# A table of ones moves from the constants to the projections' pool, and every tile on the left side of SBUF begins 96 bytes lower

## The chip, the cores and the metric

The kernel runs on one NeuronCore of a Trainium2 chip. The metric is the device time of one execution in microseconds (us). Each engine has its own instruction stream: TensorE multiplies matrices (PE in the profile, and PEld for its weight loads), VectorE (DVE) and ScalarE (ACT) work element by element, GpSimd (POOL) has a few odd jobs here, and SyncE (SP) issues the DMAs between HBM and SBUF. SBUF is the on-chip memory of 128 partitions; a tile takes the same range of bytes in each of them. PSUM takes the results of TensorE.

## The reference

Two decoder layers on one sequence of 1024 tokens with 1024 features, everything in float32. Layer 0 mixes tokens by sparse attention (an indexer scores all keys, each query keeps the best 256, then grouped attention with 16 query heads and 4 key heads of 64), layer 1 by a gated convolution of width 3. After each mixer comes a SwiGLU network with 2816 hidden features.

```python
for i in range(DEPTH):
    mod = c_act @ ada_w[i] + ada_b[i]
    sh1, sc1, g1, sh2, sc2, g2 = [m[:, None, :] for m in jnp.split(mod, 6, axis=-1)]
    h = _rmsnorm(x, norm1_g[i]) * (1.0 + sc1) + sh1
    y = _dsa_mixer(...) if i % 2 == 0 else _short_conv_mixer(...)
    x = x + g1 * y
    h = _rmsnorm(x, norm2_g[i]) * (1.0 + sc2) + sh2
    x = x + g2 * _swiglu(h, ffn_w_gate[i], ffn_w_up[i], ffn_w_down[i])

def _rmsnorm(x, g):      # used for q and k as well, over the 64 features of a head
    xf = x.astype(jnp.float32)
    y = xf * lax.rsqrt(jnp.mean(xf * xf, axis=-1, keepdims=True) + NORM_EPS)
```

## The kernel before, in words

**Layout and products.** Activations lie transposed, features on the partitions and tokens along the row, in two halves of 512 tokens. A float32 product is made of three fp32r products (`mm3`): each operand is split into a high part (a copy that rounds to fp32r, on ScalarE) and a low part (the rest, a subtraction on VectorE). The weights' parts are the tiles `whi` and `wlo`, a ring of four units each in the pool `w`; each unit is 512 columns wide, that is four 128x128 blocks, and feeds 12 matmuls. In a matmul the block of weights is loaded first (the stationary operand), and 512 columns of activations then stream past it (the moving operand). A profile's row such as `ps_g<-t,whi` names the result in PSUM, then the moving tile, then the stationary one.

**Stages.** `Attention.first_norm` and `project` make queries, keys, values and the indexer's operands (to about 294 us of the profiled span), with activations in `hhi` and `hlo`. `attend` runs the attention for eight blocks of 128 queries, and beside it the output projection (`out_tile`, moving `ohi` and `olo`), to about 622 us. `Tail.run` has the rest: the first SwiGLU network, the convolution, and the second network. There the products go by Strassen-like schemes (`Pair.done`, `down_pairs`) whose moving operands are `h11`, `h21`, `h22`, `t1` to `t4` (named `h` and `t` in rows), and `ph11` (named `ph`). In `down_pairs` the steps `m1`, `m6`, `m3`, `m5` and `m7` take the moving operand's parts from `ph`, and the steps `m2` and `m4` take them from the ring of units, so there both operands are named `whi` or `wlo`. `down` (the convolution's output projection) likewise streams units for the first half of the tokens, and for the second half parts that lie in the memory of `h22` and `t1` (rows with `rh` and `rt`).

**Order of the work.** Every instruction is first recorded and then placed by a planner (`Plan`), which keeps a clock for each engine and issues the recorded operation that can start soonest, smaller `pri` first. What it decides is fixed when the program is built.

**Places in SBUF.** A pool on the left side is put behind the pools that are open there, from low addresses upwards; a pool on the right side (`w`, `keep`, `sel`, `h`, `o`) is counted from the other end. The pool `const` is opened first, and so stands in front of all other pools of the left side: `k4` (keys), `pj` (the projections' scratch tiles), `at` (attention's), and in the tail `x2`, `u`, `h2`, `t2` and `s2`. A tile's length is rounded up to 32 bytes a partition.

**The table of ones.** `rope_pair` needs the sum of squares of each head. It multiplies the squares (`qsq`) by `blk4`, a 128x32 table that has a column of ones for each block of 32 partitions. The table is made in `setup` by one memset to zero and four memsets to one, in the pool `const`. Beside it lies `nss`, 4 numbers a partition for the tail's norms.

Of the kernel before, what the change touches and what calls it, by code (L numbers as in the profile page):

```python
# [9 lines left out]
F32 = mybir.dt.float32  # L10
# [553 lines left out]
P = 128  # L564
# [31 lines left out]
def blk(b):  # L596
    return slice(b * P, (b + 1) * P)


class Trunk:  # L600
# [111 lines left out]
    def setup(self, cz, c, positions, ada_b, n1, n2, conv_w, gq, gk, lg, lb, rope_c, arenas, kgb, freq):  # L712
        nc, cp = self.nc, self.cp
        self.ident = ident = cp.tile([P, P], F32, name="ident")
        nc.gpsimd.memset(ident, 1.0)
        nc.gpsimd.affine_select(ident, ident, pattern=[[-1, P]], compare_op=ALU.is_equal,
                                fill=0.0, base=0, channel_multiplier=1)
        self.nss = cp.tile([P, 4], F32, name="nss")
        self.blk4 = cp.tile([P, 32], F32, name="blk4")
        nc.vector.memset(self.blk4, 0.0)  # L720
        for i in range(4):
            nc.vector.memset(self.blk4[32 * i:32 * i + 32, i:i + 1], 1.0)
        rc = arenas[0].part_of(0)[0:9, P:2 * P]
        for r0, n, v in ((0, 8, c.rearrange("o (k p) -> (o k) p", p=P)), (8, 1, rope_c)):
            nc.scalar.dma_start(rc[r0:r0 + n, :], v)
        pv = self.ps("mm")
        nc.tensor.transpose(pv[:, 0:9], rc, ident[:9, :9])
        self.cact = cp.tile([P, 8], F32, name="cact")
        nc.scalar.activation(self.cact, pv[:, 0:8], AF.Silu)
        nc.vector.tensor_copy(cz[:, :, 0], self.cact)  # L730
        nc.vector.tensor_copy(freq, pv[:, 8:9])
        self.plan.pri = 1.0
        rows, rowb = arenas[0].part_of(1)[:, 0:P], arenas[1].part_of(0)[0:96, 0:P]
        nc.vector.memset(rows, 0.0)
        for r0, n, v in ((R_N1, 16, n1.rearrange("l (k p) -> (l k) p", p=P)),
                         (R_N2, 16, n2.rearrange("l (k p) -> (l k) p", p=P)),
                         (R_CW, 24, conv_w.rearrange("o w (k p) -> (o w k) p", p=P))):
            nc.sync.dma_start(rows.part_of((1, r0))[r0:r0 + n, :], v)
        nc.sync.dma_start(rowb, ada_b.rearrange("l (k p) -> (l k) p", p=P))
        g = arenas[1].part_of(96)[96:98, 0:HD]  # L740
        for r, v in enumerate((gq, gk)):
            nc.sync.dma_start(g[r:r + 1], v)
        for i, r in enumerate(R_G):
            nc.vector.tensor_copy(
                rows.part_of((1, r))[r:r + 2].rearrange("p (r q) -> p r q", q=32),
                g[:, 32 * i:32 * i + 32].unsqueeze(1).to_broadcast([2, 4, 32]))
        self.vec = vec = cp.tile([P, P], F32, name="vec")
        pv = self.ps("mm")
        read = [1] + [(1, r) for r in (R_N1, R_N2, R_CW, *R_G)]
        nc.tensor.transpose(pv[:, 0:P], rows.part_of(read), ident)  # L750
        nc.vector.tensor_copy(vec, pv[:, 0:P])
        self.adab = cp.tile([P, 96], F32, name="adab")
        pb = self.ps("mm")
        nc.tensor.transpose(pb[:, 0:96], rowb, ident[:96, :96])
        nc.vector.tensor_copy(self.adab, pb[:, 0:96])
        self.plan.pri = 27.0
        self.kgb = kgb.rearrange("p (a d) -> p a d", d=HD)
        for i, v in enumerate((lg, lb)):
            nc.sync.dma_start(self.kgb.part_of(i)[:, i], v.to_broadcast([P, HD]))
        mod = cp.tile([P, 2, 6, 8], F32, name="mod")  # L760
        self.mod = [[mod.part_of((i, j))[:, i, j] for j in range(6)] for i in range(2)]
        aff = cp.tile([P, 2, 2, 8], F32, name="aff")
        self.aff = [[aff.part_of((i, j))[:, i, j] for j in range(2)] for i in range(2)]
# [160 lines left out]
class Attention:  # L924
# [42 lines left out]


    def first_norm(self, x, positions, setup):
        tk, nc, plan, sp = self.tk, self.nc, self.plan, self.pj  # L970
        self.C, self.S = (self.hp.tile([P, T], F32, name=v) for v in "CS")
        plan.pri = 0.0
        cz = self.score[7][:, 0:HW].part_of("c").rearrange("p (k m) -> p k m", m=HD)
        nc.vector.memset(cz, 0.0)
        setup(cz, (self.C, self.S))
        self.kp.tile([P, 32], F32, name="pad")
        xt = [self.kp.tile([P, KT, HW], F32, name="xt%d" % i, tag="k%d" % i) for i in range(NH)]
# [101 lines left out]
    def project(self):  # L1079
        tk, nc, sp, plan = self.tk, self.nc, self.pj, self.plan  # L1080
# [2 lines left out]
            "p (h t) -> p h t", h=IH // 2)  # L1083
        self.ssk = sp.tile([P, TB, KVH], F32, name="ssk", bufs=1)
        self.wiT = sp.tile([P, TB, IH], F32, name="wiT", bufs=1)
        n, s, ends = HD + IH, 0, []
        kw = self.s4()
        self.plan.pri = self.KI_W
# [58 lines left out]
        for b in range(TB):  # L1147
            ps = tk.ps("mm", "gemm")[:, 0:KVH * HD]
# [19 lines left out]
    def rope_pair(self, w, half, ts, col, ss, s):  # L1168


        tk, nc, sp = self.tk, self.nc, self.pj
        n = ts.stop - ts.start
        ab, sqs = [], []
        for two in range(2):
            self.unit(s)
            ps = tk.gemm_tile(w[two], P, self.h[half], ts=ts)
            t = sp.tile([P, HW], F32, name="rt", tag="rt")[:, 0:n]
            if col is None:
                self.plan.copy(t, ps)
            else:  # L1180
                c = R_G[two] + col
                nc.scalar.activation(t, ps, AF.Copy, scale=tk.vec[:, c:c + 1])
            if ss is not None:
                sq = sp.tile([P, HW], F32, name="qsq", tag="t2")
                nc.scalar.activation(sq, ps, AF.Square)
                sqs.append(sq)
            ab.append(t)
            s += 1
        if ss is not None:
            ps = tk.ps("mm", "sq")  # L1190
            self.plan.matmuls([(ps.part_of(g)[32 * g:32 * g + 32, 0:P], tk.blk4, sq[:, blk(g)])
                               for sq in sqs for g in range(4)], 3.5e-3, side=4)
            row = sqs[0][:, 0:P]
            self.plan.copy(row, ps.part_of([0, 1, 2, 3])[:, 0:P])
            sm = ps.part_of("n")[:, P:P + 16]
            nc.tensor.matmul(sm, row, tk.ident.rearrange("p (g q) -> p g q", q=32)[:, :, 0:4],
                             start=True, stop=True)
            nc.vector.tensor_copy(ss[:, half * 4:half * 4 + 4, :],
                                  sm.rearrange("p (t n) -> p t n", n=4))
        sl = slice(half * HW + ts.start, (half + 1) * HW)  # L1200
        tmp = [sp.tile([P, HW], F32, name="sw", tag="sw")[:, 0:n] for _ in range(2)]
        tk.rotate(ab, tmp, self.C[:, sl], self.S[:, sl])
        return ab, sl, s
# [892 lines left out]
```

## Time and profile before

| what | value |
|---|---|
| median of 3 runs | 2287.76 us (2282.33 to 2289.04) |
| the profiled execution's own time | 2281.89 us |
| its span, first to last instruction | 2280.1 us |
| PE busy | 2228.1 us, 98% of the span |
| DVE busy | 1903.0 us, 83% |
| ACT busy | 1138.9 us, 50% |
| DMA, q1 | 350.48 MB, 48.5% of 16 engines' span |

A row of a grouped view reads: line, engine, operation, output tile, inputs, shapes, count, then the busy time in us and the mean of one in ns, then the engine's idle time ahead of these instructions and what ended it. Matmuls overlap and their ends are modelled, so the mean duration of one is longer than the time from one start to the next. The rate at which TensorE goes is therefore read from starts: from the timeline, or from the number of matmuls in a window.

### The profile page before, as it was taken

What the parts mean: (1) busy time and instruction counts of PE and PEld (TensorE: products, weight loads), DVE (VectorE), ACT (ScalarE), POOL (GpSimd) and SP (SyncE); (2) the same over time, 40 slices, a digit from 0 to 9 for tenths busy, and PEclk for the clock granted to TensorE, in tenths of its full rate; (3) what the DMA queues carried; (4) which work ended last, traced back from release to release, by engine and by line L of the source; (5) the groups of instructions that cost most, each with busy time, mean ns of one, the idle gap of its engine ahead of it and who ended that gap; (6) DMA issues with size and microseconds to landing.
All of it is one profiled execution on the core that took longest, in us unless ns stands there. A gap on an engine that the chain in (4) does not pass through costs nothing.

```text
span 2280.1 us, 32466 instructions
## 1 busy us (share of the span) xinstructions
PE 2228.1 (98%) x11319; PEld 1761.1 (77%) x11319; DVE 1903.0 (83%) x3888; ACT 1138.9 (50%) x2183; POOL 4.5 (0%) x19
## 2 busy tenths in 40 slices
PE   7999989999999999999999999999999999999999
PEld 4757867887888778888888787787888888888887
DVE  6899999797798898888897999886888876768874
ACT  5578899978563233333445642234553333334444
POOL 0000000000000000000000000000000000000000
PEclk9999989999999999999999999999999999999999
DMA  9303343522555655548971544244436432349724
GB/s 334 115 19 93 107 116 91 151 82 68 161 154 176 205 179 166 168 146 288 376 237 64 162 117 147 84 122 137 139 97 195 157 107 89 117 148 388 265 83 139
DMA packets 332542, 352.68 MB, mean 155 GB/s; under 512 B 20025, under 2 KB 217690, under 8 KB 332378
## 3 DMA queue, kind: packets, MB, share of 16 engines
q1 hardware_dynamic: 332168, 350.48, 48.5%
q8 instruction: 88, 1.44, 0.3%
q14 instruction: 76, 0.62, 0.1%
q10 hardware_dynamic: 210, 0.14, 0.0%
HBM read 278.97 MB, written 68.94 MB: 153 GB/s over the span
## 4 chain that ended last, share of the span: by engine, by line
PE 78%; DVE 9%; issue 6%; ACT 4%; DMA 2%; SPq 0%; ACTq 0%; POOL 0%; POOLq 0%; DVEq 0%
PE ps_g L282 46%; PE ps_mm L282 29%; PE ps_o L282 2%; DVE u L282 1%; DVE s L282 1%; PE ps_L L282 1%; DVE wlo L282 1%; ACT p L282 1%; DMA adaw<-in_ada_w_dram 1%; ACT pf L282 1%; DVE p L282 1%; DVE karena L282 1%; DVE adacc L282 1%; DVE sc L282 1%; ACT karena L282 1%
## 5 line engine op out<-in xcount | busy, mean ns | idle before, releaser
L282 ACT CAST whi<-raw 128x512 fp32r<-128x512 f32 x310 | 191.5, 621 | 400.8 <-PE ps_g L282 163.0
L282 PE MATMUL ps_g<-t,whi 128*128 128x512 f32 x1184 | 373.8, 397 | 1.9 <-ACT whi L282 1.9
L282 ACT CAST whi<-s 128x512 fp32r<-128x512 f32 x276 | 170.6, 620 | 334.5 <-PE ps_g L282 138.7
L282 PE MATMUL ps_g<-h,whi 128*128 128x512 f32 x1056 | 333.0, 396 | 1.6 <-ACT whi L282 1.6
L282 DVE TENSOR_TENSOR wlo<-raw,whi 128x512 fp32r<-128x512 f32 x312 | 213.9, 686 | 79.4 <-ACT whi L282 78.0
L282 PEld LDWEIGHTS ps_g<-t,whi 128*128 128x128 f32 x1184 | 222.4, 188 | 55.5 <-ACT whi L282 3.0
L282 PE MATMUL ps_g<-t,wlo 128*128 128x512 f32 x592 | 234.6, 396 | 2.5 <-DVE wlo L282 2.4
L282 PEld LDWEIGHTS ps_g<-h,whi 128*128 128x128 f32 x1056 | 197.6, 188 | 49.5 <-ACT whi L282 2.9
L282 PE MATMUL ps_g<-h,wlo 128*128 128x512 f32 x528 | 208.5, 396 | 0.0
L282 DVE TENSOR_TENSOR wlo<-s,whi 128x512 fp32r<-128x512 f32 x276 | 187.8, 686 | 19.2 <-ACT whi L282 18.8
L282 PE MATMUL ps_mm<-t,whi 128*128 128x512 f32 x608 | 193.0, 397 | 2.1 <-ACT whi L282 2.0
L282 PE MATMUL ps_g<-ph,whi 128*128 128x512 f32 x572 | 181.5, 394 | 0.0
L282 PEld LDWEIGHTS ps_mm<-t,whi 128*128 128x128 f32 x608 | 114.8, 189 | 30.8 <-ACT whi L282 3.4
L282 PEld LDWEIGHTS ps_g<-t,wlo 128*128 128x128 f32 x592 | 111.4, 188 | 32.3 <-DVE wlo L282 4.7
L282 PEld LDWEIGHTS ps_g<-ph,whi 128*128 128x128 f32 x572 | 107.3, 188 | 25.9
L282 PE MATMUL ps_mm<-t,wlo 128*128 128x512 f32 x304 | 121.1, 398 | 2.0 <-DVE wlo L282 2.0
L282 ACT ACTIVATE junk<-sc,bs 128x896 bf16<-128x896 f32 (+3 forms) x124 | 110.0, 887 | 16.9 <-DVE bs L282 8.0
L282 PEld LDWEIGHTS ps_g<-h,wlo 128*128 128x128 f32 x528 | 99.2, 188 | 24.7 <-DVE wlo L282 0.4
L282 DVE TENSOR_TENSOR u<-u 128x512 f32<-128x512 f32 x170 | 114.3, 685 | 3.4 <-ACT u L282 2.5
L282 PE MATMUL ps_g<-ph,wlo 128*128 128x512 f32 x286 | 112.9, 396 | 0.0
L282 DVE SCALAR_TENSOR_TENSOR adacc<-adaw,cact,adacc 128x512 f32<-128x512 f32 x140 | 104.4, 746 | 7.8 <-DMA adaw<-in_ada_w_dram 7.3
L282 PE MATMUL ps_mm<-ph,whi 128*128 128x512 f32 x308 | 97.7, 394 | 0.0
(333 smaller groups left out, 4640.2 us busy)
## 6 DMA issues: line engine op xcount, KB each, us to landing
adaw<-in_ada_w_dram SPq DMA_DIRECT2D x160, 256.0 KB, 3.2
ph<-in_ffn_w_down_dram SPq DMA_DIRECT2D x66, 512.0 KB, 6.0
raw<-in_ffn_w_gate_dram SPq DMA_DIRECT2D x54, 512.0 KB, 4.2
raw<-in_ffn_w_up_dram SPq DMA_DIRECT2D x54, 512.0 KB, 4.1
raw<-in_conv_w_in_dram SPq DMA_DIRECT2D x34, 512.0 KB, 4.2
raw<-in_ffn_w_down_dram SPq DMA_DIRECT2D x44, 256.0 KB, 2.7
ph<-in_ffn_w_down_dram SPq DMA_DIRECT2D x44, 256.0 KB, 4.1
raw<-in_attn_w_in_dram SPq DMA_DIRECT2D x18, 512.0 KB, 4.2
```

What stands on the lines that cost most here:

```text
L282: f(*[a.get() if isinstance(a, Ref) else a for a in args], **{k: a.get() if isinstance(a, Ref) else a for k, a in kw.items()})
```

## The change

`blk4` is made in the pool `pj` when `project` is recorded, and `nss` asks for 16 numbers a partition of which 4 are used. All the computation is the same.

```diff
@@ setup
-        self.nss = cp.tile([P, 4], F32, name="nss")
-        self.blk4 = cp.tile([P, 32], F32, name="blk4")
-        nc.vector.memset(self.blk4, 0.0)
-        for i in range(4):
-            nc.vector.memset(self.blk4[32 * i:32 * i + 32, i:i + 1], 1.0)
+        self.nss = cp.tile([P, 16], F32, name="nss")[:, 0:4]
@@ project
         self.wiT = sp.tile([P, TB, IH], F32, name="wiT", bufs=1)
+        self.blk4 = sp.tile([P, 32], F32, name="blk4", bufs=1)
+        nc.vector.memset(self.blk4, 0.0)
+        for i in range(4):
+            nc.vector.memset(self.blk4[32 * i:32 * i + 32, i:i + 1], 1.0)
@@ rope_pair
-            self.plan.matmuls([(ps.part_of(g)[32 * g:32 * g + 32, 0:P], tk.blk4, sq[:, blk(g)])
+            self.plan.matmuls([(ps.part_of(g)[32 * g:32 * g + 32, 0:P], self.blk4, sq[:, blk(g)])
```

**Instructions.** Buffer numbers aside, the streams of PE, ACT, POOL and SP are the same rows in the same order, and their waits are the same. On DVE one row moves, at the very start of the program (`sc` is a zeroed operand of the conditioning, `C` a staging area for small inputs, `blk` the table, `bs` a state of the key selection). Before:

```order
L282 MEMSET sc_247 128x512
L282 MEMSET blk_85 128x32
L282 MEMSET C 128x128
L282 TENSOR_SCALAR bs<-bs 128x2
L282 MEMSET blk_85 32x1 x4
L282 TENSOR_SCALAR bs<-bs 128x2 x2
```

And with the change:

```order
L282 MEMSET sc_246 128x512
L282 MEMSET C 128x128
L282 MEMSET blk_279 128x32
L282 TENSOR_SCALAR bs<-bs 128x2
L282 MEMSET blk_279 32x1 x4
L282 TENSOR_SCALAR bs<-bs 128x2 x2
```

The memset to zero of the table has gone behind that of `C`; its four memsets to one stay where they were.

**Addresses.** `nss` and `blk4` took 32 + 128 bytes of each partition, and `nss` now takes 64. So all that follows on the left side begins 96 bytes lower, and since 96 = 64 + 32, what began at a multiple of 64 now begins 32 bytes past one, and the other way round. In `pj` the table then takes its 128 bytes behind `wiT`, which shifts nothing but a few small tiles there. The right side stays. As the two programs are built, the first byte in a partition:

| tiles (pool) | before | after | modulo 64, before and after |
|---|---|---|---|
| `h11`, `ph11` (h2) | 52800 | 52704 | 0, 32 |
| `h21`, into which `down_pairs` loads weights (h2) | 69184 | 69088 | 0, 32 |
| `h22`, `t1`, `t2`, `t3`, `t4` (t2) | 85568, 101952, 118336, 134720, 151104 | each 96 less | 0, 32 |
| `xr` (x2) | 7360 | 7264 | 0, 32 |
| `s`, 4 buffers (s2); `adaw` (t2) | 196512 on; 192416, 194464 | each 96 less | 32, 0 |
| `ks`, the keys' parts (k4) | 23872 | 23776 | 0, 32 |
| `p`; `pf` (at) | 40352 on; 57056 on | each 96 less | 32, 0 |
| `whi`, `wlo`, 4 buffers each (w) | 212960 on | the same | 32, 32 |
| `raw`, 2 buffers (w) | 204768 on | the same | 32, 32 |
| `hhi`, `hlo` (h); `ohi`, `olo` (o) | 107744 on, 74976 on; 91360, 115936 | the same | 32, 32 |
| `ident` (const) | 5248 | the same | 0, 0 |

The slices of these tiles that a matmul streams begin whole multiples of 64 bytes further on, so they share the tile's remainder.

## The prediction

> **What bounds the kernel now.** I read the page first, then the matmuls grouped by shape, then windows of the steady stretches, then the timeline of TensorE where two kinds of moving operand meet. The page says that TensorE sets the end:
>
> ```profile
> span 2280.1 us, 32466 instructions
> PE 2228.1 (98%) x11319; PEld 1761.1 (77%) x11319; DVE 1903.0 (83%) x3888; ACT 1138.9 (50%) x2183; POOL 4.5 (0%) x19
> PE ps_g L282 46%; PE ps_mm L282 29%; PE ps_o L282 2%; DVE u L282 1%; DVE s L282 1%; PE ps_L L282 1%; DVE wlo L282 1%; ACT p L282 1%; DMA adaw<-in_ada_w_dram 1%; ACT pf L282 1%; DVE p L282 1%; DVE karena L282 1%; DVE adacc L282 1%; DVE sc L282 1%; ACT karena L282 1%
> ```
>
> Three quarters of the chain that ended last are matmuls into `ps_g` and `ps_mm`. So the question is whether a matmul costs the same after the change. The next view groups them; these twelve are the tail's products that stream `t`, `h` and `ph`.
>
> ```profile
> L282 PE MATMUL ps_g<-t,whi 128*128 128x512 f32 x1184 | 373.8, 397 | 1.9 <-ACT whi L282 1.9
> L282 PE MATMUL ps_g<-h,whi 128*128 128x512 f32 x1056 | 333.0, 396 | 1.6 <-ACT whi L282 1.6
> L282 PE MATMUL ps_g<-t,wlo 128*128 128x512 f32 x592 | 234.6, 396 | 2.5 <-DVE wlo L282 2.4
> L282 PE MATMUL ps_g<-h,wlo 128*128 128x512 f32 x528 | 208.5, 396 | 0.0
> L282 PE MATMUL ps_mm<-t,whi 128*128 128x512 f32 x608 | 193.0, 397 | 2.1 <-ACT whi L282 2.0
> L282 PE MATMUL ps_g<-ph,whi 128*128 128x512 f32 x572 | 181.5, 394 | 0.0
> L282 PE MATMUL ps_mm<-t,wlo 128*128 128x512 f32 x304 | 121.1, 398 | 2.0 <-DVE wlo L282 2.0
> L282 PE MATMUL ps_g<-ph,wlo 128*128 128x512 f32 x286 | 112.9, 396 | 0.0
> L282 PE MATMUL ps_mm<-ph,whi 128*128 128x512 f32 x308 | 97.7, 394 | 0.0
> L282 PE MATMUL ps_mm<-h,whi 128*128 128x512 f32 x288 | 90.9, 396 | 0.0
> L282 PE MATMUL ps_mm<-ph,wlo 128*128 128x512 f32 x154 | 61.1, 397 | 0.0
> L282 PE MATMUL ps_mm<-h,wlo 128*128 128x512 f32 x144 | 56.7, 394 | 0.0
> ```
>
> Their counts sum to 2688 for `t`, 2016 for `h` and 1320 for `ph`: 6024. With the 192 matmuls of `down` that stream `rh` and `rt` from the same memory (8 f times 8 d times 3), 6216 matmuls of 128x512 stream an operand that begins at a multiple of 64 bytes, and the change moves each of them 32 bytes past one. Their modelled durations (394 to 398 ns) overlap, so the rate has to come from counts. In the following windows the columns are the stretch, its length, then busy time and count for PE, PEld, DVE, ACT and POOL, the granted clock, the DMA share and GB/s. The first two stretches stream `ph`, and `t` and `h`. The third and fourth are inside the down projection's last two steps and the convolution's output projection, where the ring's `whi` and `wlo` are streamed. The fifth, in the projections, streams `hhi` and `hlo`. The last three tiles begin at 32 modulo 64.
>
> ```profile
> 1068.00:1218.00 150.00, 150.00 (x645) 120.67 (x644) 126.31 (x201) 64.69 (x113) 0.00 (x0) 1.00 0.78 278
> 1840.00:2040.00 200.00, 200.00 (x859) 160.90 (x858) 141.96 (x224) 68.56 (x116) 0.00 (x0) 1.00 0.31 102
> 1224.00:1251.00 27.00, 27.00 (x120) 22.29 (x119) 23.12 (x37) 14.07 (x26) 0.00 (x0) 1.00 0.28 90
> 1531.00:1574.00 43.00, 43.00 (x191) 35.58 (x190) 25.07 (x40) 19.46 (x35) 0.00 (x0) 1.00 0.55 182
> 73.00:83.00 10.00, 10.00 (x46) 8.27 (x45) 9.76 (x29) 2.55 (x6) 0.00 (x0) 1.00 0.40 117
> ```
>
> TensorE is busy throughout in all five, at full clock. A window counts each matmul that overlaps it, and with 0.39 us for one matmul that is about 1.7 more than start in it. So one matmul takes 150/643.3 = 233.2 ns and 200/857.3 = 233.3 ns in the first two, and 27/118.3 = 228.2, 43/189.3 = 227.2 and 10/44.3 = 225.7 ns in the others. Same shape, type, clock and weights' ring, two rates. The timeline of TensorE, where a last group with `ph` is followed by products from the ring (start, us, operation):
>
> ```profile
> 1220.99 0.63 PE L282 MATMUL ps_g<-ph,whi 128*128 128x512 f32 x2
> ...
> 1223.81 0.40 PE L282 MATMUL ps_mm<-whi 128*128 128x512 f32 x1
> ...
> 1229.74 0.39 PE L282 MATMUL ps_mm<-whi,wlo 128*128 128x512 f32 x1
> ```
>
> From 1220.99 to 1223.81 there are 12 starts, 235.0 ns each; from 1223.81 to 1229.74 there are 26, 228.1 ns each. The rate changes with the operand, within one stage. What the tiles at 233 ns have in common is the place: `h11` to `t4`, all over the left side, begin at 0 modulo 64. The quick ones begin at 32. Height in SBUF doesn't part them (`t4` at 151104 has the long gap, `ohi` at 91360 and `hhi` at 107744 lie between such tiles), nor does load: DMA share 0.31 and 0.78 go with 233 ns, 0.28 and 0.55 with 227 to 228. Whether the absolute address counts or its distance to the weights (which lie at 32 in all these cases) can't be told here; after the change both say the short gap.
>
> A rule speaks against this. The Trainium skill, TensorE: Matmul & The Clock Gate, in "Wait — 56ns, not 53.3ns?", gives start-to-start once warm as the columns over 2.4 GHz plus about 2.5 ns, 215.7 ns for 512 columns, with no word of an address; by it the change is worth nothing. The trace does not agree, with 233 and 228 ns for one shape at one clock. The Trainium skill, SBUF — State Buffer, in "Operand start alignment", treats alignment as a matter of what is legal and says that its runs timed nothing, so it doesn't decide.
>
> **The change part by part.** *The five memsets.*
>
> ```profile
> 1.42 0.09 DVE L282 MEMSET blk<- 128x32 f32 x1
> 1.71 0.35 DVE L282 MEMSET blk<- 32x1 f32 x4
> 6.62 0.69 DVE L282 COPY xt<-ps_mm 128x512 f32<-128x512 f32 x1 [4.14 <-PE ps_mm L282]
> ```
>
> They are the same five instructions, one of them a place later. All are done by 2.1 us and VectorE then stands idle for 4.14 us waiting for TensorE, so the term is 0; without that cover it would be the 0.09 us of the moved row. The table's new place serves as weights of small matmuls and `nss` keeps its four numbers: 0.
>
> *The moving operands of the tail.* The saving per matmul lies between 5.0 ns (233.2 less 228.2) and 6.1 ns (233.3 less 227.2). I leave out the ten-microsecond window, too short for its edges. I take 5.6: 6216 x 5.6 ns = 34.8 us off TensorE's work (31.1 to 37.9).
>
> *What others give back.* TensorE is not ahead everywhere. These are its waits between 620 and 2232 us, then two windows in which it stalls and one in which it doesn't, and then ScalarE's first split of a weight unit in the first of the two and in a steady stretch (740 to 840 and 1760 to 2060 us):
>
> ```profile
> PE ps_g L282 <- ACT whi L282: 3.9, 5, 1.4
> PE ps_g L282 <- DVE wlo L282: 3.0, 3, 1.4
> 740.00:840.00 100.00, 94.83 (x399) 74.13 (x398) 89.48 (x149) 29.37 (x50) 0.00 (x0) 0.98 0.62 200
> 1340.00:1480.00 140.00, 136.44 (x574) 107.37 (x573) 127.68 (x224) 35.30 (x59) 0.00 (x0) 0.99 0.38 109
> 1640.00:1740.00 100.00, 100.00 (x430) 80.48 (x429) 88.75 (x145) 44.92 (x77) 0.00 (x0) 1.00 0.46 134
> L282 ACT CAST whi<-s 128x512 fp32r<-128x512 f32 x24 | 14.8, 620 | 33.5 <-DVE s L282 32.9 <-ACT u L282 0.3
> L282 ACT CAST whi<-s 128x512 fp32r<-128x512 f32 x63 | 39.1, 621 | 91.6 <-PE ps_g L282 63.2 <-PE ps_mm L282 20.9 <-issue 4.9
> ```
>
> In the steady stretch ScalarE sits idle until TensorE frees a unit of the ring (84 of 91.6 us): the ring is full, and whatever TensorE saves stays saved. From 740 to 840 us it waits for VectorE's sums instead (32.9 of 33.5), VectorE is busy for 89.48 of 100 us, and TensorE idles. There, and from 1340 to 1480 us (127.68 of 140), VectorE sets the pace, and a faster matmul only lengthens the wait for `whi` and `wlo`. They hold 399 + 574 = 973 matmuls: 973 x 5.6 = 5.4 us given back. For places where the ring runs low without a stall today (as at the pairs of steps `m6`, `m3`, with VectorE at 126.31 of 150 us) I add 2 us. Bounds: 0, if the earlier gains let VectorE run ahead as well, and 12, if as many matmuls again are held up.
>
> *Attention.* `pf` goes the other way, from 32 to 0, and `ks` from 0 to 32.
>
> ```profile
> L282 PE MATMUL ps_o<-pf,vst 128*64 128x128 f32 x1152 | 75.6, 279 | 2.4 <-ACT pf L282 1.7 <-ACT on L282 0.5
> L282 PE MATMUL ps_L<-ks,qs 64*128 64x512 f32 x288 | 45.2, 423 | 1.5 <-DVE mx L282 1.4
> ```
>
> If the whole 5.6 ns fell on each pass over `pf`, that would be a loss of 6.5 us; by its length, a quarter of the columns, 1.6. `ks` has 288 matmuls of 512 columns which run as pairs on two row halves: 0.8 to 1.6 us gained, and as much again at most for its shorter ones. I take 0, with ends of 6.5 lost and 3.2 gained.
>
> *DMAs.* No DMA is added. `s` and `adaw` now land at multiples of 64, `xr`, the half of `h2` that takes weights, and the rows for `down_pairs` at 32; `raw` always landed at 32:
>
> ```profile
> ph<-in_ffn_w_down_dram SPq DMA_DIRECT2D x44, 256.0 KB, 4.1
> raw<-in_ffn_w_down_dram SPq DMA_DIRECT2D x44, 256.0 KB, 2.7
> ```
>
> The same matrix in pieces of the same size lands in 2.7 us at 32 and 4.1 us at 0, in different steps. Nothing says that 32 is worse: 0.
>
> *The sum.* 34.8 - 5.4 - 2 = 27.4 us less than the profiled execution's own 2281.9 us (span 2280.1): 2254.5. The median of the runs shown, 2287.8, lies 5.9 above that execution; half of it added gives **2257 us**.
>
> **The rivals.** *VectorE takes more of it.* For: it is busy for 88.75 of 100 us from 1640 to 1740 and 126.31 of 150 from 1068 to 1218, where nothing stalls yet. If these two and the two stretches above are all paced by it, they hold 645 + 399 + 574 + 430 = 2048 matmuls or 11.5 us, and if as much again is lost in stretches like them, 11.8 us of gain remain: 2270, with the 3 us added 2273. Against: VectorE would have to be within 2.4% of full there, and in the steady stretch it is at 141.96 of 200. *The address is not the cause.* Then the two rates come from something else that `whi`, `hhi` and `ohi` share, and nothing moves: 2282 to 2288. For: no row shows one tile at both places. Against: five tiles with the long gap and three kinds with the short one, in all stages. The Trainium skill's rule, TensorE: Matmul & The Clock Gate, would give the same. *Landings get slower at 32*, the other side: in `down_pairs` the DMA share is 0.78 from 1068 to 1218 and it is there twice. If transfers to 32 took 1.28 times as long, DMA would be the bound; at 1.5 times the two stretches of about 150 us would grow by 0.17 each, 51 us, against 27 gained: 2254.5 + 51 = 2306, and from 1.40 on the kernel is slower than before (300 x 0.09 = 27). Against: the landing of `raw` above. *Nothing is given back*, and the saving is 6.1 ns: 2281.9 - 37.9 = 2244.
>
> **How the numbers follow.** Forecast (20 to 35 us gained) 0.71; VectorE takes more 0.13; nothing given back 0.05; address not the cause 0.07; slower landings 0.04. The range reaches from the case without loss, 2244, nearly to the one where VectorE takes more, 2272, which leaves out the last two cases and about half of the second. A change of 0.3% (7 us) is what a measurement here can tell from none: faster 0.71 + 0.13 + 0.05 = 0.89, same 0.07, slower 0.04.
>
> **What would show it.** Right: windows over `t`, `h` and `ph` count a matmul every 227 to 228 ns, as those over `whi` do; TensorE's waits for `whi` and `wlo` grow by some 5 us around 760 and 1380 us; the landing times stay. Wrong: the rate over `t` is still 233 ns, or it is 228 and the windows of 100 us with VectorE near 90 show idle time of TensorE, or the passes over `pf` become longer by more than 1.4 ns each.

## The result, and the profile after

The changed kernel takes 2247.97 us (median of 4 runs, 2245.95 to 2250.06) against 2286.24 us for the kernel before (4 runs, 2282.33 to 2289.04): a ratio of 0.9834 with a 95% interval of 0.9815 to 0.9852, 38.3 us less. The forecast was 2257 us (2244 to 2272). The profiled execution of the changed kernel took 2250.06 us.

The head of the page after, and the start of the chain that ended last: the same instructions, TensorE still the bound, and its busy time 34.3 us shorter (2228.1 before).

```profile
span 2248.3 us, 32466 instructions
PE 2193.8 (98%) x11319; PEld 1762.2 (78%) x11319; DVE 1897.4 (84%) x3888; ACT 1141.7 (51%) x2183; POOL 4.5 (0%) x19
PE ps_g L282 43%; PE ps_mm L282 29%; DVE u L282 2%; DVE wlo L282 2%; PE ps_o L282 2%; DVE s L282 2%; PE ps_L L282 1%; DMA adaw<-in_ada_w_dram 1%; DVE karena L282 1%; DVE p L282 1%; DVE adacc L282 1%; DVE v L282 1%; DVE sc L282 1%; DMA xr<-xs 1%; ACT p L282 0%
```

The windows of the kernel after, columns as in the prediction. The first two stream `ph`, and `t` and `h`; the next two hold the products that stream the ring's own units; the last three are the stretches in which VectorE is busiest.

```profile
1062.00:1206.00 144.00, 144.00 (x635) 118.59 (x634) 123.38 (x199) 65.12 (x111) 0.00 (x0) 1.00 0.82 292
1820.00:2020.00 200.00, 200.00 (x884) 165.68 (x883) 142.99 (x226) 68.48 (x116) 0.00 (x0) 1.00 0.35 112
1212.00:1240.00 28.00, 28.00 (x125) 23.18 (x125) 24.22 (x39) 16.04 (x30) 0.00 (x0) 1.00 0.27 85
1517.00:1559.00 42.00, 42.00 (x187) 34.80 (x186) 24.11 (x38) 19.14 (x34) 0.00 (x0) 1.00 0.55 182
740.00:840.00 100.00, 93.62 (x405) 73.93 (x404) 90.92 (x152) 29.54 (x50) 0.00 (x0) 1.00 0.63 203
1340.00:1480.00 140.00, 136.05 (x586) 109.62 (x585) 127.35 (x223) 34.68 (x58) 0.00 (x0) 0.99 0.40 118
1640.00:1740.00 100.00, 100.00 (x443) 82.84 (x442) 88.63 (x146) 43.03 (x73) 0.00 (x0) 1.00 0.50 148
```

With 1.7 taken off each count as before, a matmul over `ph` now takes 144/633.3 = 227.4 ns (233.2 before), and one over `t` and `h` 200/882.3 = 226.7 ns (233.3 before). The two stretches that had the short gap already keep it: 28/123.3 = 227.1 and 42/185.3 = 226.7 ns. Every 128x512 product of the tail now goes at one rate, within 1 ns.

Where the 38 us lie shows at two points of TensorE's timeline (start, duration, operation): the first product that streams `h`, which begins the tail, and the transposes of `xr` late in the last `down_pairs`. First the kernel before, then after.

```profile
621.74 0.63 PE L282 MATMUL ps_g<-h,whi 128*128 128x512 f32 x2
...
2232.01 0.60 PE L282 MATMUL ps_mm<-ident,xr 128*128 128x128 f32 x4
```

```profile
626.15 0.62 PE L282 MATMUL ps_g<-h,whi 128*128 128x512 f32 x2
...
2199.96 0.60 PE L282 MATMUL ps_mm<-ident,xr 128*128 128x128 f32 x4
```

The tail between them took 1610.3 us before and 1573.8 after: 36.5 us less. What stands ahead of it took 4.4 us more in this one execution, and what follows takes 48.1 and 48.3 us. So the two profiled executions differ by 31.8 us in span, while the medians differ by 38.3: the one before was 4.4 us under its median, the one after 2.1 us over its own.

The 4.4 us ahead of the tail are lost in attention, where the granted clock was at half for longer: from its first product over `ks` to the tail it took 335.3 us before, 339.9 in this execution of the changed kernel and 335.6 in another execution of it. One window, first of the kernel before, then of after, then of the same kernel run again (an experiment below):

```profile
312.00:324.00 12.00, 10.47 (x104) 7.29 (x100) 12.00 (x43) 12.00 (x37) 0.00 (x0) 1.00 0.36 89
```

```profile
312.00:324.00 12.00, 11.84 (x70) 7.86 (x70) 8.49 (x27) 8.63 (x27) 0.00 (x0) 0.58 0.33 89
```

```profile
312.00:324.00 12.00, 10.48 (x95) 6.96 (x93) 11.95 (x46) 12.00 (x38) 0.00 (x0) 1.00 0.35 89
```

The granted clock is 0.58 here in the execution after, and 1.00 in the other two. The half clock ended at 309.8 us before, at 322.1 in this execution of the changed kernel and at 311.4 in the other; over all the kernels below it ended anywhere from 307 to 325 us. Two executions of one program differ as much as the two programs do, so the change isn't needed to explain it. The Trainium skill, TensorE: Matmul & The Clock Gate, in "What's actually happening", says that the window by which the clock is opened runs freely and does not restart with a kernel, so that the moment of the change differs from run to run. It puts that variation at 500 ns either way; between the two executions here the end of the half clock differs by 10.7 us, so that rule alone doesn't account for it, and what does stays open.

### The profile page after: what moved, and what is told of

Its sections match the earlier page's. It is cut to its first block, busy times and chain, and to the rows that moved or that the text cites. A ratio compares the mean times of both kernels' runs of the same rounds, so it can differ in the third digit from the quotient of the medians.

```text
span 2248.3 us, 32466 instructions
## 1 busy us (share of the span) xinstructions
PE 2193.8 (98%) x11319; PEld 1762.2 (78%) x11319; DVE 1897.4 (84%) x3888; ACT 1141.7 (51%) x2183; POOL 4.5 (0%) x19
## 4 chain that ended last, share of the span: by engine, by line
PE 75%; DVE 12%; issue 6%; DMA 4%; ACT 2%; SPq 0%; POOL 0%; ACTq 0%; DVEq 0%; POOLq 0%
PE ps_g L282 43%; PE ps_mm L282 29%; DVE u L282 2%; DVE wlo L282 2%; PE ps_o L282 2%; DVE s L282 2%; PE ps_L L282 1%; DMA adaw<-in_ada_w_dram 1%; DVE karena L282 1%; DVE p L282 1%; DVE adacc L282 1%; DVE v L282 1%; DVE sc L282 1%; DMA xr<-xs 1%; ACT p L282 0%
## 5 line engine op out<-in xcount | busy, mean ns | idle before, releaser
L282 PE MATMUL ps_g<-t,whi 128*128 128x512 f32 x1184 | 366.4, 391 | 2.3 <-ACT whi L282 2.3
L282 PE MATMUL ps_g<-h,whi 128*128 128x512 f32 x1056 | 326.5, 390 | 1.8 <-ACT whi L282 1.6
L282 PE MATMUL ps_mm<-t,whi 128*128 128x512 f32 x608 | 188.3, 390 | 2.3 <-ACT whi L282 2.1
L282 PEld LDWEIGHTS ps_mm<-t,whi 128*128 128x128 f32 x608 | 114.0, 188 | 27.4 <-ACT whi L282 4.0
```

The source lines that it names most:

```text
L282: f(*[a.get() if isinstance(a, Ref) else a for a in args], **{k: a.get() if isinstance(a, Ref) else a for k, a in kw.items()})
```

## The experiments

One quantity orders most of them: the distance **d**, the first byte of the moving operand less the first byte of the ring's units (`whi`, `wlo`), modulo 256. Before, `t`, `h` and `ph` begin at 64 modulo 256 and the units at 224, so d = 96. After, both begin at 224 and d = 0. `hhi`, `hlo`, `ohi`, `olo` and a streamed unit had d = 0 already. The diffs against the kernel after, or before where said, are cut to what counts.

**1. The addresses put back.** The kernel after with a longer `nss`, so that all on the left side returns to where it was, while the table stays in its new pool and its memset in its new place.

```diff
-        self.nss = cp.tile([P, 16], F32, name="nss")[:, 0:4]
+        self.nss = cp.tile([P, 40], F32, name="nss")[:, 0:4]
```

> The changed kernel, but nss takes 160 bytes a partition, so that all addresses of the left side are those of before while the table stays in the projections' pool and the memsets in their new order. If the start address of the moving operand is the cause: matmuls over t, h and ph every 233 ns again, and the time of before, 2282 to 2289 us. If the table's place or the order of the memsets were the cause: 2246 to 2250 us and 227 ns.

Measured: 2284.88 us (10 runs, 2281.70 to 2289.46), ratio to before 0.9999 (0.9989 to 1.0010). The window over `t` and `h`:

```profile
1840.00:2040.00 200.00, 200.00 (x859) 160.89 (x858) 141.93 (x225) 66.51 (x113) 0.00 (x0) 1.00 0.33 105
```

200/857.3 = 233.3 ns again. The whole gain hangs on the addresses; the table's pool and the order of the memsets are worth nothing that these runs can tell.

**2. Only the tail's tiles, by 32 bytes.** The kernel before, with 32 bytes ahead of `h11`: `h11` to `t4` and `ph` move from 0 to 32 modulo 64 (d from 96 to 128), `s` and `adaw` from 32 to 0, and everything else stays.

```diff
@@ the tail's pools, in the kernel before
         self.sp = Pool(plan, "s2", bufs=4)
+        self.bp.tile([P, 8], F32, name="pad")
```

> The kernel before with a tile of 32 bytes put in front of h11 in the pool h2: only h2, t2 and s2 move, by +32 bytes, so h11 to t4 begin at 32 modulo 64 and keys, attention, xr and u stay where they were before. If the moving operands of the tail are the whole cause: 227 ns a matmul, the tail 36 us shorter, 2247 to 2252 us. The attention's 4 us that the changed kernel's profile lost between 310 and 322 us: if its addresses did that, this one is about 4 us below the changed kernel (2244); if chance, the same as it. If other left tiles (xr, u, ks, p, pf) carry a good part of the gain: 2255 to 2275.

Measured: 2281.11 us (10 runs), ratio 0.9986 (0.9976 to 0.9997).

```profile
1840.00:2040.00 200.00, 200.00 (x863) 162.13 (x862) 141.40 (x224) 67.03 (x113) 0.00 (x0) 1.00 0.32 105
```

200/861.3 = 232.2 ns, 1.1 less than before and 5.5 more than after. This expectation failed clearly: the tiles begin at 32 modulo 64, as all the tiles with the short gap did, and the gap stays long. "32 modulo 64" is not the cause, whether it is read as an address or as an equal remainder with the weights.

**3 and 4. The weights moved instead.** 32 bytes at the end of pool `w` move the whole right side down by 32, so the units begin at 192 modulo 256. Experiment 3 does it to the kernel before (d = 64 - 192, that is 128), experiment 4 to the kernel after (d = 32).

```diff
@@ unit
+        u = [...]                      # the same two tiles as before
+        if not self.padded:
+            self.padded = self.wp.tile([P, 8], F32, name="pad", tag="pad", bufs=1)
+        return u
```

> The kernel before with 32 bytes more at the end of the pool w, so that the right side (weights' units, hhi, hlo, ohi, olo) begins at 0 modulo 64, as the tail's moving operands do. If the moving operand's own address counts: everything at 233 ns, windows over whi too; 2016 more matmuls at 5.5 ns: 2286 + up to 11 = 2288 to 2297 us. If the distance to the weights counts (equal remainders are quick): 227 ns over t, h and ph, some 36 us less, 2246 to 2254 us.

> The changed kernel with the same 32 bytes in w: moving t, h, ph at 32, weights at 0; moving whi, hhi, ohi and the weights both at 0. Own address: t at 227 ns, whi, hhi and ohi at 233; 2248 + up to 11 = 2250 to 2259 us. Distance: t at 233, whi at 227, 2282 to 2289 us.

Measured: 2279.92 us (10 runs), ratio 0.9976 (0.9967 to 0.9986), for experiment 3, and 2283.71 us (10 runs), ratio 0.9996 (0.9987 to 1.0005), for experiment 4. The first met neither theory. Its window over `t` and `h` has the long gap of before, 200/857.3 = 233.3 ns:

```profile
1840.00:2040.00 200.00, 200.00 (x859) 160.94 (x858) 141.84 (x224) 68.00 (x115) 0.00 (x0) 1.00 0.32 102
```

The second shows most: `t`, `h` and `ph` are where the changed kernel has them, and its gain is gone. Its timeline in the down projection, where `ph` streams and then units do:

```profile
1225.65 0.63 PE L282 MATMUL ps_g<-ph,whi 128*128 128x512 f32 x2
...
1228.45 0.40 PE L282 MATMUL ps_mm<-whi 128*128 128x512 f32 x1
...
1231.21 0.39 PE L282 MATMUL ps_mm<-whi 128*128 128x512 f32 x1
...
1236.65 0.39 PE L282 MATMUL ps_mm<-whi 128*128 128x512 f32 x1
```

From 1225.65 to 1228.45 there are 12 starts, 233.3 ns each, over `ph` at 224 modulo 256. Behind the first product over units (12 starts at 230.0 ns), from 1231.21 to 1236.65, there are 24 starts, 226.7 ns each, over units that now begin at 192, that is at 0 modulo 64, with weights at the same remainder. A place of its own doesn't set the gap. What the cases with the short gap have in common is that operand and weights begin at the same remainder modulo 256; that the same remainder modulo 64 is not enough, experiment 2 has shown.

**5. A ruler.** The kernel after with 32 bytes between the seven operands of the networks, each of which gets a name of its own. `ha`, `hb`, `hc`, `ta`, `tb`, `tc` and `td` lie at d = -32, 0, 32, 64, 96, 128 and 160, in one program and against the same units.

```diff
@@ operand
+        if name not in self.b and name != "h11":
+            pool.tile([P, 8], F32, name="pad" + "abcdefg"[len(self.b)])
...
-        self.nss = cp.tile([P, 16], F32, name="nss")[:, 0:4]
+        self.nss = cp.tile([P, 4], F32, name="nss")
```

> The changed kernel with nss back at 32 bytes and 32 bytes put between the tail's seven operand tiles, so that their starts lie at -32 (ha, in place of h11, and ph), 0 (hb, h21), 32 (hc, h22), 64 (ta, t1), 96 (tb, t2), 128 (tc, t3) and 160 bytes (td, t4) from the weights' units, modulo 256. If equal remainders modulo 256 make a matmul quick: 227 ns over hb alone and 232 to 234 over the six others, 2276 to 2284 us. If a matmul is quick at several distances, or the cost grows with the distance: rates that differ among ha, hc, ta, tb, tc, td, down to 227 at some.

Measured: 2279.24 us (5 runs), ratio 0.9971 (0.9956 to 0.9986). TensorE's timeline in the steady stretch; each row shown begins a product of 12 matmuls, and the next row begins the next product.

```profile
1890.42 0.63 PE L282 MATMUL ps_g<-ha,whi 128*128 128x512 f32 x2
...
1893.22 0.62 PE L282 MATMUL ps_g<-hb,whi 128*128 128x512 f32 x2
...
1895.94 0.63 PE L282 MATMUL ps_mm<-td,whi 128*128 128x512 f32 x2
...
1898.75 0.63 PE L282 MATMUL ps_g<-ta,whi 128*128 128x512 f32 x2
...
1901.51 0.63 PE L282 MATMUL ps_g<-tb,whi 128*128 128x512 f32 x2
...
1904.31 0.63 PE L282 MATMUL ps_mm<-hc,whi 128*128 128x512 f32 x2
...
1907.11 0.62 PE L282 MATMUL ps_g<-tc,whi 128*128 128x512 f32 x2
...
1909.89 0.63 PE L282 MATMUL ps_g<-ha,whi 128*128 128x512 f32 x2
```

Each difference divided by 12, good to about 1 ns, and beside it the mean over all starts with that operand from 1700 to 2060 us of the same trace (144 to 244 of them):

| operand | d modulo 256 | ns from start to start, one product | mean, 1700 to 2060 us |
|---|---|---|---|
| `hb` | 0 | 226.7 | 227.3 |
| `hc` | 32 | 233.3 | 233.1 |
| `ta` | 64 | 230.0 | 229.4 |
| `tb` | 96 (as in the kernel before) | 233.3 | 234.1 |
| `tc` | 128 | 231.7 | 231.7 |
| `td` | 160 | 234.2 | 233.8 |
| `ha` | 224 (-32) | 233.3 | 232.6 |

Only d = 0 gives the short gap. 64 gives about half of the gain and 128 about a quarter. Experiments 2 and 3 both have d = 128, and their windows give 232.2 and 233.3 ns; in 3, operand and units both lie 32 bytes lower than in 2. So off d = 0 the distance alone doesn't fix the gap to the nanosecond, and what else has a part in it stays open. A distance of 192 was not measured. That 256 is the period, and not a larger number, shows in the kernel before: `ohi` lies 121600 bytes below the units, 475 times 256, an odd multiple. The timeline of its output projection:

```profile
606.10 0.39 PE L282 MATMUL ps_mm<-ohi,whi 128*128 128x512 f32 x1
...
612.90 0.39 PE L282 MATMUL ps_mm<-ohi,whi 128*128 128x512 f32 x1
```

These are 30 starts in 6.80 us, 226.7 ns each.

**6. The units stay, the rest of the right side moves.** The kernel after with 32 bytes between `raw` and the units, so that `hhi`, `hlo`, `ohi` and `olo` move to d = -32 while the tail keeps d = 0.

```diff
@@ raw
-        return self.wp.tile([P, D], F32, name="raw", tag="raw")
+        t = self.wp.tile([P, D], F32, name="raw", tag="raw")
+        if not self.padded:
+            self.padded = self.wp.tile([P, 8], F32, name="pad", tag="pad", bufs=1)
+        return t
```

> The changed kernel with 32 bytes put between raw and the units in the pool w: whi and wlo stay where they are, and everything else of the right side (raw, hhi, hlo, ohi, olo, the attention's qs) goes 32 bytes down. If the distance of the streamed operand to the weights counts: t, h, ph and whi at 227 ns as in the changed kernel, hhi, hlo, ohi and olo at 233 (960 matmuls of 512 columns: up to 5 us more), 2248 to 2255 us. If the distance to raw or another right-side tile counts: t, h and ph at 233, 2281 to 2289 us.

Measured: 2254.30 us (4 runs, 2252.42 to 2258.88), ratio 0.9865 (0.9848 to 0.9881). The window over `t` and `h`, and two rows of the output projection:

```profile
1840.00:2040.00 200.00, 200.00 (x885) 165.58 (x884) 145.22 (x230) 70.91 (x120) 0.00 (x0) 1.00 0.41 135
```

```profile
611.86 0.40 PE L282 MATMUL ps_mm<-ohi,whi 128*128 128x512 f32 x1
...
618.86 0.40 PE L282 MATMUL ps_mm<-ohi,whi 128*128 128x512 f32 x1
```

The tail keeps its 226.4 ns (200/883.3), and `ohi` goes from 226.7 to 7.00/30 = 233.3 ns: the effect taken away from tiles that always had it, in another stage and on the other side of SBUF. The 384 matmuls of the output projection make 2.5 us of the loss of 6 us against the changed kernel's 2247.97. `hhi` and `hlo`, streamed by 576 more in the projections, go from 228 to 233 ns on the mean of their starts, up to 3 us if nothing there waits for another engine; the rest was not taken apart.

**7. Finer than 32 bytes.** The kernel after with the tail's tiles moved so that `h21` (here `hb`) begins at d = 4, `h11` (`ha`) at d = -16, `h22` and `t1` to `t4` at d = 32, and `ph` at d = -32. `n` and `at` pick the tile's name and its first element.

```diff
@@ operand, for h11 (at = 4) and h21 (at = 1); 32 bytes more a tile
+            t = self.bp.tile([P, 8 * HW + 8], F32R, name=n, tag=name)[:, at:at + 8 * HW]
...
-        self.nss = cp.tile([P, 16], F32, name="nss")[:, 0:4]
+        self.nss = cp.tile([P, 4], F32, name="nss")
```

> The changed kernel with nss at 32 bytes and the two operand tiles of h2 longer by 32 bytes, in which h11 begins 16 bytes in (16 below the weights modulo 256; named ha) and h21 4 bytes in (4 above; named hb); ph lies 32 below and h22 and t1 to t4 32 above. If the starts must agree to the byte: 232 to 234 ns everywhere. If only the 32-byte (or 16-byte) line counts: 227 over hb, and over ha 233.

Measured: 2289.29 us (8 runs), ratio 1.0020 (1.0010 to 1.0031). Three products in a row on the timeline:

```profile
1896.60 0.63 PE L282 MATMUL ps_g<-t,whi 128*128 128x512 f32 x2
...
1899.40 0.63 PE L282 MATMUL ps_g<-ha,whi 128*128 128x512 f32 x2
...
1902.20 0.63 PE L282 MATMUL ps_g<-hb,whi 128*128 128x512 f32 x2
...
1905.06 0.62 PE L282 MATMUL ps_mm<-t,whi 128*128 128x512 f32 x2
```

`ha` at -16 takes 2.80/12 = 233.3 ns, and `hb`, one float past the weights' remainder, 2.86/12 = 238.3 ns, the longest gap of all. A distance of one float is worse here than one of 32 bytes, so coming near doesn't help: of what was tried, only the equal remainder has the short gap.

**8 and 9. Two controls.** Experiment 8 keeps the tail's tiles where the change puts them and everything of the left side ahead of them (keys, attention, `xr`, `u`) 32 bytes lower. Experiment 9 is the changed kernel again, without an edit.

```diff
@@ experiment 8
-        self.nss = cp.tile([P, 16], F32, name="nss")[:, 0:4]
+        self.nss = cp.tile([P, 4], F32, name="nss")
...
         self.sp = Pool(plan, "s2", bufs=4)
+        self.bp.tile([P, 8], F32, name="pad")
```

> The changed kernel with nss at 32 bytes and 32 bytes put in front of h11: h2, t2 and s2 lie as in the changed kernel, and keys, the projections' scratch, attention, xr and u 32 bytes lower. Tail at 227 ns a matmul. If the place of the attention's tiles makes the half clock at 290 us last to 322 us (as in the changed kernel, against 307 to 310 where they lie elsewhere): about 4 us below the changed kernel, 2243 to 2246 us. If that length is chance: the same as the changed kernel, 2246 to 2250.

> The changed kernel once more, beside the one before it on this list: 2246 to 2250 us, and 322 us again for the end of the half clock if its addresses set it, another value if it is chance.

Measured: 2247.96 us (4 runs), ratio 0.9836 (0.9823 to 0.9850), and 2245.28 us (5 runs), ratio 0.9827 (0.9813 to 0.9840). What moved ahead of the tail counts for nothing that can be measured, and the result repeats: the 2.7 us between the two lie within the spread of one program's runs. The half clock ended at 323.2 us in experiment 8, with attention's tiles in another place, and at 311.4 in experiment 9, so that place doesn't set its end.

**10. Units of two remainders.** The kernel after with 32 bytes between the `whi` and the `wlo` units: `wlo` stays at 224, where `t`, `h` and `ph` begin, and `whi` moves to 192. `raw`, `hhi`, `hlo`, `ohi` and `olo` move to 192 with it. It asks whether what counts is a matmul's own weights or those loaded for the next one while it streams.

```diff
@@ unit
+        u = [self.wp.tile([P, HW], F32R, name="whi", tag="whi", bufs=self.UNITS)]
+        if not self.padded:
+            self.padded = self.wp.tile([P, 8], F32, name="pad", tag="pad", bufs=1)
+        return u + [self.wp.tile([P, HW], F32R, name="wlo", tag="wlo", bufs=self.UNITS)]
```

> The changed kernel with 32 bytes between whi and wlo in the pool w: wlo stays at 224 modulo 256 as t, h and ph have it, whi goes to 192. Each triple in order is high part on whi, low part on whi, high part on wlo. If a matmul's own weights count: the first two of a triple take 233 ns and the one on wlo 227. If the weights that are loaded while it streams count (those of the matmul behind it): the second takes 227, the first and third 233. Either way some 693 ns a triple and two thirds of the gain lost, 2270 to 2280 us.

Measured: 2292.98 us (5 runs, 2290.54 to 2293.93), ratio 1.0031 (1.0019 to 1.0044).

```profile
1840.00:2040.00 200.00, 200.00 (x859) 161.02 (x858) 141.62 (x224) 66.85 (x113) 0.00 (x0) 1.00 0.32 104
```

200/857.3 = 233.3 ns on the mean, as with all weights at a distance. By their place in the triple (`whi`, `whi`, `wlo`) the mean gaps over `t` in the whole trace are 235.7, 233.1 and about 231 ns. Both forms of the theory wanted a matmul of the triple at 227; none comes there. So the gain needs one remainder for all the weights and the operand. The time, above the 2270 to 2280 us expected, also holds what other streams lose that now meet weights of two remainders: a unit streamed from the ring takes 232 ns on the mean of its starts, where it took 227 to 228. Which reads meet each other in the machine stays open: no run here separates it further.

## Why the prediction was right, and where it wasn't

The direction and the place held, and so did the mechanism as far as this: the gap over `t`, `h` and `ph` hangs on the address, the change shortened it, and TensorE set the end. Which addresses have the short gap was read wrongly (below). Each step:

- **The saving per matmul** was sized too low. Forecast 5.6 ns, between 5.0 and 6.1; measured 233.3 - 226.7 = 6.6 ns over `t` and `h` and 233.2 - 227.4 = 5.8 ns over `ph`. With 2688 + 2016 + 192 = 4896 matmuls of the one kind and 1320 of the other that is 32.3 + 7.7 = 40.0 us, where 34.8 stood (31.1 to 37.9). The fault was in the choice of the rows for the short gap: 228.2 came from a window of 27 us with changes of operand in it, while the output projection, in the kernel before's own timeline, had 226.7 ns over 30 starts.
- **What others give back** was sized too high. The forecast was 7.4 us (0 to 12); of the 40.0 us the tail kept 36.5, so 3.5 came back. TensorE's waits in the tail, as they are after, with `nr` as it was before:

```profile
PE ps_g L282 <- ACT whi L282: 4.5, 6, 1.3
PE ps_g L282 <- DVE wlo L282: 3.6, 4, 1.5
PE ps_mm L282 <- DVE nr L282: 2.1, 1, 2.1
```

```profile
PE ps_mm L282 <- DVE nr L282: 1.3, 1, 1.3
```

They grew by 0.6, 0.6 and 0.8 us, 2.0 in all, where some 5 had been said for `whi` and `wlo`. The place was right (the window from 740 to 840 us has 93.62 us of TensorE after 94.83), the amount was not: not every matmul of a stretch in which VectorE is busy is paced by it. From 1640 to 1740, with VectorE at 88.63 of 100 us, TensorE does not idle at all, which also ends the rival in which VectorE takes more. The remaining 1.5 us aren't attributed.
- **Attention** as nothing held, though one sign named for a wrong prediction shows: the passes over `pf` take 281 ns on the mean after 279, and more than 1.4 ns had been called such a sign. That is 0.9 us over 1152 of them. The row of `ks` is 422 after 423:

```profile
L282 PE MATMUL ps_o<-pf,vst 128*64 128x128 f32 x1152 | 76.5, 281 | 2.7 <-ACT pf L282 1.7 <-ACT on L282 0.8
L282 PE MATMUL ps_L<-ks,qs 64*128 64x512 f32 x288 | 45.0, 422 | 1.5 <-DVE mx L282 1.4
```

The 2 ns lie ahead of 340 us, where the half clock lasted longer in this execution, and not in the address. From 340 to 620 us `pf` has the same mean, first before and then after (and in experiment 9, the changed kernel with the shorter half clock, the mean over all of them is 279 again):

```profile
L282 PE MATMUL ps_o<-pf,vst 128*64 128x128 f32 x1032 | 64.7, 276 | 0.0
```

```profile
L282 PE MATMUL ps_o<-pf,vst 128*64 128x128 f32 x1035 | 65.1, 276 | 0.0
```

These are modelled durations. That the addresses cost nothing that can be measured rests on experiment 8, which moves `pf` and `ks` and takes 2247.96 us.

- **Landings** as nothing held, and the rival on the other side fell:

```profile
raw<-in_ffn_w_down_dram SPq DMA_DIRECT2D x44, 256.0 KB, 2.8
ph<-in_ffn_w_down_dram SPq DMA_DIRECT2D x44, 256.0 KB, 4.1
```

These are 2.8 after 2.7 and 4.1 after 4.1 us, with the mean DMA share at 0.82 from 1062 to 1206 us. The larger pieces for `ph` (66 of 512 KB) took 6.8 us after 6.0, but 6.6 in experiment 1, which has the addresses of before; no wait of TensorE in the tail is put down to a DMA.

- **The memsets** as nothing are confirmed by experiment 1.
- **From the profiled execution to the median**: the 3 us added were right in kind, but the execution after had its own deviation, 4.4 us of half clock ahead of the tail, and stood 2.1 us over its median.

The sum with measured terms: 2281.9 - 40.0 + 3.5 + 4.4 + 0.2 = 2250.0, the time of the profiled execution after. The tail's gain was 9.1 us larger than forecast (36.5 for 27.4): 5.2 from the saving and 3.9 from what comes back. That is nearly all of the distance from 2257 to 2248.

**The reading that failed** is the sentence on what the tiles at 233 ns have in common: they "begin at 0 modulo 64. The quick ones begin at 32." It was true of every row and is not the cause. The prediction left open whether the address or its distance to the weights counts, and experiment 4 decides for the distance. But it took 64 as the period for both, and experiment 2 refutes that. By the same argument a shift of 32 bytes would have been forecast to gain as much as the shift of 96, and it gains 0.14%. That the forecast came out right was luck in this respect: 96 bytes is the one shift, among multiples of 32 below 256, that takes 64 modulo 256 to the weights' 224. All the tiles with the short gap had one remainder modulo 256, and all the others had one other: with two places only, any period that parts them fits.

The rule that was weighed, the Trainium skill, TensorE: Matmul & The Clock Gate, "Wait — 56ns, not 53.3ns?", gives 215.7 ns for 512 columns, with no word of an address. The same shape at full clock took 226.7, 230.0, 231.7, 233.3, 234.2 and 238.3 ns in one kernel or another here, by address alone. The Trainium skill, on the same page, in "Step-by-step: what each phase is for", says that weights and streaming operand have separate read ports, so that loading the next weights takes nothing from the matmul that runs. The runs don't bear that out as it stands: moving the right side by 32 bytes, in the tail the weights' units and `raw`, in experiment 4, took the gap over `t`, `h` and `ph` from 227 to 233 ns. Where the two reads meet, no run shows.

## What to carry to other kernels

Where 128x512 fp32r matmuls with a weight load each are the bound, compare the gap from start to start (from counts or timelines, not from modelled durations) between tiles, and give the streamed operand the same first byte modulo 256 as all the weights that it meets: here 226.7 against 233.3 ns, 1.7% of the kernel, for a few bytes of padding. Such a layout breaks whenever a pool ahead changes its length, as experiment 1 shows, so it should be set by the tiles' own padding and looked at again after each change of the memory plan. And where two groups of tiles differ in speed and in place, a second place for one of them (a ruler as in experiment 5) tells the rule from the coincidence before it is built on.

## What the runs showed of the hardware that wasn't expected

- The start-to-start time of a 128x512 fp32r matmul with a load of weights ahead of it depends mainly on the distance of its two SBUF addresses modulo 256: 226.7 ns at 0, 230.0 at 64, 231.7 to 233.3 at 128, 233 to 234 at 32, 96, 160 and 224, and 238.3 at 4.
- With weights of two remainders in turn the mean gap is 233.3 ns, as without any that agree; even the matmuls whose own weights agree take about 231 ns and not 227 (2292.98 us in all).
- The half clock at the start of attention ended between 307 and 325 us of the span, in two executions of one program at 311.4 and 322.1 us.
